# Addresses at multiples of 512 bytes for the large on-chip buffers of a two-layer decoder trunk

## The chip, the cores and the metric

The kernel runs on one core of one Trainium2 chip. The metric is the device time of one execution in microseconds (us); three runs of the kernel before took 2226.89 to 2227.21 us, median 2227.1. A core has TensorE (matrix products, PE in the profile, with its weight loads as PEld), VectorE (DVE), ScalarE (ACT), GpSimd (POOL) and SyncE (SP). The on-chip memory SBUF has 128 partitions; an address below is the byte offset within a partition, the same in all of them. Products are accumulated in another memory, PSUM.

## The reference

256 tokens of width 2048 in float32 pass two layers.

```python
h = x
for layer in range(2):
    hn = rms_norm(h, norm_mix[layer])
    if layer == 0:
        mix = recurrent_mixers(hn, ...)     # RG-LRU scan beside HGRN2 heads, then w_out
    else:
        mix = dilated_attention(hn, positions, w_qkv, w_o)   # rotary on 32 of 128 features
    h = h + mix
    h = h + relu(rms_norm(h, norm_mlp[layer]) @ w1[layer]) ** 2 @ w2[layer]
return rms_norm(h, final_norm)
```

All weights (about 410 MB) are read once. HGRN2 works in chunks by masks of a triangular recurrence; the attention turns the first 32 features of queries and keys by angles made from `positions`.

## The kernel before

*Products.* Each float32 operand is split in two float32r parts, hi (a rounded copy, ScalarE, L104) and lo (the rest, VectorE, L105), and a product is the sum of three: hi with hi, hi with lo, lo with hi. Activations stand split in `bufa` and `bufb`, 16 blocks of 128 features, each with 256 columns of hi and 256 of lo. Every product of a weight with an activation is issued on line 176, by `mm`, which keeps TensorE's order. There are two directions. `project` makes features times tokens: 128 columns of the weights' `hi` or `lo` are stationary, and a block of `bufa` moves, 512 columns (both parts) with hi, 256 with lo (`cross`, L208), or 256 three times (`direct`, L214). `tokens` and `products` make tokens times features: 128 columns of `bufa`, `bufb` or `forms` are stationary and 512 columns of `hi` or `lo` move. `forms` holds sums of blocks, with which `products` does a 2 by 2 block product of w2 in seven block products instead of eight.

*Weights.* They come as units of 1 MB, [128, 2048] float32, in a fixed order (`units`). Each goes by a transfer on SP's queue to one of three buffers `raw`, and is split to one of three `hi` and three `lo`. `fetch` runs two units ahead of use. `raw` is free for the next transfer when VectorE has written `lo`. For `products`, units are also combined: `a` and `t1` lie in a pool `pair`, opened after the recurrence, and POOL's queue adds to `t1` by a transfer (L138).

*Places.* A pool takes a range of SBUF in the order of the `tile_pool` calls, and its buffers the places in order of first use. The default is a multiple of 32 bytes; `align_bytes=LINE`, 64 here, is asked for by bufa, bufb, hi, lo and forms. Closing a pool (`mixers.close()`, `pairs.close()`) frees its range for the next, whose first writers then wait for the last users.

*Around the change.* The scan masks `msk` (L249) lie in the constants' pool and are loaded on POOL's queue at the start; the masked copies of `hgrn` (L474) read them. `nr` of pool `tmp` holds the row of inverse norms `rs` (L365), by which each projection of the layer is multiplied (L411); one buffer of this name, first for layer 0, later for layer 1. `ppi` (L726) is a buffer of the pool `rot`, opened when the recurrence's pool has been closed; positions come to it by a DMA of POOL's queue, and fifteen VectorE operations (L731 to L750) and two sines on ScalarE make `cosT` and `sinT`, which are first used in the attention. A scheduler orders each engine's instructions by its own estimate of time; `urgent` and `stream` raise a priority. `lru_gates` runs its products into three PSUM buffers `p`, which the readers (L199, L411) free again.

Of the kernel before, what the change touches and what calls it, by code (L numbers as in the profile page):

```python
# [10 lines left out]
F32 = mybir.dt.float32  # L11
F32R = mybir.dt.float32r
BF16 = mybir.dt.bfloat16
I32 = mybir.dt.int32
# [5 lines left out]
P = 128  # L20
S = 256
D = 2048
KB = D // P
EPS = 1e-6
LEVELS = (1, 2, 4, 8, 16)
NLEV = len(LEVELS)
# [14 lines left out]
def trunk_kernel(ctx, tc, x, xtok, cols, tab, masks, pos, fin, w_in, w_gate, w_out, w_qkv, w_o, w1, w2, out):  # L41
    nc = tc.nc
    pool = lambda name, bufs=1, **kw: ctx.enter_context(tc.tile_pool(name=name, bufs=bufs, **kw))
    cst = pool("cst")
    act = pool("act")
    wraw = pool("wraw", 3)
    whi = pool("whi", 3)
    wlo = pool("wlo", 3)
    tmp = pool("tmp", 2)
# [8 lines left out]
    xall = act.tile([P, KB * S], F32, name="xall")  # L58
    xin = xall.rearrange("p (k s) -> p k s", s=S)
    xres = xall.rearrange("p (j d) -> p j d", j=2)  # L60
    bufa = act.tile([P, KB, 2 * S], F32R, name="bufa", align_bytes=LINE)
    bufb = act.tile([P, KB, 2 * S], F32R, name="bufb", align_bytes=LINE)

    units = []
    made = {}
# [27 lines left out]
    class Weights:  # L93
        def __init__(self, raw, step=2048):
            self.raw = raw
            self.hi = whi.tile([P, 2048], F32R, name="hi", align_bytes=LINE)
            self.lo = wlo.tile([P, 2048], F32R, name="lo", align_bytes=LINE)
            for at in range(0, 2048, step) if step else ():
                self.split(at, step)

# [145 lines left out]
        fetch_first()  # L246
    tab_ = cst.tile([P, NTAB], F32, name="tab_")
    nc.gpsimd.dma_start(tab_, tab)
    msk = cst.tile([P, NLEV, P], mybir.dt.int8, name="msk")  # L249
    nc.gpsimd.dma_start(msk, masks)  # L250
    ident = tab_[:, TC_ID:TC_ID + P]
    lnc = tab_[:, TC_LNC:TC_LNC + 384]
    epsc = cst.tile([P, 1], F32, name="epsc")
# [168 lines left out]

    vgs = mixers.enter_context(tc.tile_pool(name="vgs", bufs=1))
    wk = mixers.enter_context(tc.tile_pool(name="wk", bufs=2))


    def halves(t, c, second):
# [150 lines left out]
    rot = mixers.enter_context(tc.tile_pool(name="rot", bufs=1))  # L578
# [140 lines left out]
    pair = pairs.enter_context(tc.tile_pool(name="pair0", bufs=1))  # L719
    forms = pair.tile([P, 4, 2, 512], F32R, name="forms", align_bytes=LINE)  # L720
    nx1 = Norm()
# [1 line left out]
    pairs.close()  # L723


    ppi = rot.tile([32, S], I32, name="ppi")  # L726
    nc.gpsimd.dma_start(ppi, bass.AP(tensor=pos.tensor, offset=pos.offset, ap=[[0, 32], [1, S]]))
    ang = rot.tile([32, S], F32, name="ang")
    cosT = rot.tile([32, S], F32, name="cosT")
# [24 lines left out]
    wk = mixers.enter_context(tc.tile_pool(name="wk2", bufs=2))  # L754
# [69 lines left out]
    pair = pairs.enter_context(tc.tile_pool(name="pair1", bufs=1))  # L824
    forms = pair.tile([P, 4, 2, 512], F32R, name="forms", align_bytes=LINE)
    fnorm = Norm()
# [25 lines left out]
URGENT = 400  # L852
ORDER = "v0 h0 x0 h1 x1 h2 x2 h3 x3 v1 h4 x4 h5 x5 h6 x6 h7 x7 g0 y0 y1 y2 y3 g1 y4 y5 y6 y7"
WARM = 12
LINE = 64
PAIRS = 2
T3_DMA = True
PRODUCTS = (("a", 0), ("t1", 4), ("n", 6), ("t2", 5), ("c", None), ("n", 7), ("t3", None), ("d", 1),
# [105 lines left out]
```

## Time and profile before

| | |
|---|---|
| median of three runs | 2227.1 us |
| the profiled execution | 2227.31 us, of which its span 2225.5 |
| instructions | 29702 |
| granted TensorE clock, mean | 0.998 |
| read from HBM | 427.48 MB, 193 GB/s over the span |
| transfers on SP's queue | 52.8% of 16 engines' span |
| VectorE, line 105 (lo) | 822.1 us |
| ScalarE, line 104 (hi) | 688.3 us |

Shares of time are of the span. The groups of the page have busy time, the mean of one, and the idle time before them with what ended it. A stretch of the chain of waits has its start, its length and what worked. In the order in time the first column is the start, the second the time until the last of the merged instructions ended; products are pipelined, so one starts before the one before has drained, and the distance between starts tells the pace. In the busy time by stretches, each engine's time has the number of its instructions behind it.

### The profile page before, as it was taken

How to read it: one execution, taken by the hardware profiler on the slowest of the kernel's cores; microseconds unless marked ns; L12 is line 12 of the kernel's file. 1: busy time of each engine (PE TensorE's matmuls, PEld its weight loads, DVE VectorE, ACT ScalarE, POOL GpSimd, SP SyncE). 2: the span in 40 equal slices, each digit the busy share in tenths (PEclk: the TensorE clock that was granted, in tenths of full speed). 3: DMA queues.
4: the chain of work that ended last, by engine and by line, in shares of the span. 5: the costliest groups of instructions: out<-in, count | busy, mean ns of one | idle time of the engine just before them, and what ended most of it. 6: DMA issues, size and time to landing. Idle time of an engine off the chain costs nothing.

```text
span 2225.5 us, 29702 instructions
## 1 busy us (share of the span) xinstructions
PE 2207.2 (99%) x12004; PEld 1892.6 (85%) x12004; DVE 1673.0 (75%) x2286; ACT 1110.0 (50%) x1364; POOL 15.8 (1%) x23
## 2 busy tenths in 40 slices
PE   9999999999999999999999999999999999999997
PEld 8999998888888888888888888888878888888886
DVE  8777796578777877877867878556787687687787
ACT  6444585444445444544654444444454454454454
POOL 0000000000000000000000000000000000000000
PEclk9999999999999999999999999999999999999999
DMA  8444446556655755755654544655566567566553
GB/s 312 163 158 163 158 154 228 180 185 203 229 187 186 242 196 174 244 199 159 208 207 158 182 173 164 224 179 185 158 218 241 171 201 247 188 189 246 190 189 114
DMA packets 61017, 431.25 MB, mean 194 GB/s; under 512 B 6784, under 2 KB 7552, under 8 KB 9424
## 3 DMA queue, kind: packets, MB, share of 16 engines
q1 hardware_dynamic: 58320, 412.20, 52.8%
q0 software_dynamic: 2560, 17.16, 4.2%
q8 instruction: 94, 1.54, 0.3%
q14 instruction: 43, 0.35, 0.0%
HBM read 427.48 MB, written 2.10 MB: 193 GB/s over the span
## 4 chain that ended last, share of the span: by engine, by line
PE 95%; DVE 3%; ACT 1%; DMA 0%; issue 0%; SPq 0%; ACTq 0%; DVEq 0%
PE p L176 81%; PE po L176 6%; PE pd L176 5%; DVE lo L105 1%; PE pl L471 1%; ACT hi L104 1%; PE pl L179 0%; DVE a L142 0%; PE pl L777 0%; PE po L798 0%; DMA xall<-in_x 0%; PE pd L790 0%; DMA a<-in_w 0%; DVE bufa L234 0%; PE pd L455 0%
## 5 line engine op out<-in xcount | busy, mean ns | idle before, releaser
L105 DVE TENSOR_TENSOR lo<-raw,hi 128x1024 fp32r<-128x1024 f32 (+2 forms) x486 | 822.1, 1709 | 359.3 <-ACT hi L104 339.2
L104 ACT CAST hi<-raw 128x1024 fp32r<-128x1024 f32 (+2 forms) x486 | 688.3, 1441 | 685.2 <-PE p L176 524.9
L176 PE MATMUL p<-bufa,hi 128*128 128x512 f32 (+1 forms) x3840 | 862.8, 359 | 2.4 <-DVE bufa L234 2.3
L176 PEld LDWEIGHTS p<-bufa,hi 128*128 128x128 f32 x3840 | 668.1, 188 | 104.8 <-DVE bufa L234 3.8
L176 PE MATMUL p<-bufa,lo 128*128 128x256 f32 x3200 | 517.6, 283 | 0.0
L176 PEld LDWEIGHTS p<-bufa,lo 128*128 128x128 f32 x3200 | 449.4, 188 | 14.2
L176 PE MATMUL p<-hi,bufb 128*128 128x512 f32 x1408 | 458.0, 395 | 0.2 <-DVE xall L650 0.2
L176 PEld LDWEIGHTS p<-hi,bufb 128*128 128x128 f32 x1408 | 264.4, 188 | 64.1 <-DVE xall L650 3.1
L176 PE MATMUL p<-lo,bufb 128*128 128x512 f32 x704 | 277.8, 395 | 0.3 <-DVE lo L105 0.2
L104 ACT CAST hi<-a 128x2048 fp32r<-128x2048 f32 x64 | 122.0, 1906 | 160.9 <-PE p L176 83.6
L105 DVE TENSOR_TENSOR lo<-a,hi 128x2048 fp32r<-128x2048 f32 x64 | 146.5, 2289 | 55.5 <-ACT hi L104 55.4
L176 PEld LDWEIGHTS p<-lo,bufb 128*128 128x128 f32 x704 | 132.1, 188 | 33.1 <-DVE lo L105 2.7
L176 PE MATMUL p<-hi,bufa 128*128 128x512 f32 x384 | 125.1, 400 | 0.4 <-ACT hi L104 0.4
L176 PEld LDWEIGHTS p<-hi,bufa 128*128 128x128 f32 x384 | 72.3, 188 | 16.7 <-ACT hi L104 1.3
L176 PE MATMUL pd<-hi,bufb 128*128 128x512 f32 x256 | 85.5, 395 | 0.1
L176 PE MATMUL po<-hi,bufb 128*128 128x512 f32 x256 | 85.4, 394 | 0.1
L176 PE MATMUL p<-hi,forms 128*128 128x512 f32 x256 | 85.4, 394 | 0.0
L176 PE MATMUL p<-lo,bufa 128*128 128x512 f32 x192 | 76.5, 399 | 1.8 <-DVE lo L105 1.8
L142 DVE TENSOR_TENSOR a<-a,raw 128x2048 f32<-128x2048 f32 x32 | 73.0, 2282 | 0.0
L223 ACT COPY t<-p 128x256 f32<-128x256 f32 x128 | 47.0, 367 | 41.4 <-PE p L176 41.1
L650 DVE SCALAR_TENSOR_TENSOR xall<-p,nm,xall 128x512 f32<-128x512 f32 x64 | 47.7, 746 | 24.7 <-PE p L176 24.7
L230 ACT CAST bufb<-zp 128x256 fp32r<-128x256 f32 x128 | 50.8, 404 | 17.2 <-DVE zp L684 17.1
(239 smaller groups left out, 1807.9 us busy)
## 6 DMA issues: line engine op xcount, KB each, us to landing
raw<-in_w SPq DMA_DIRECT2D x224, 1024.0 KB, 4.8
raw<-in_w_qkv SPq DMA_DIRECT2D x48, 1024.0 KB, 4.8
raw<-in_w_in SPq DMA_DIRECT2D x46, 1024.0 KB, 4.8
raw<-in_w_out SPq DMA_DIRECT2D x16, 1024.0 KB, 4.8
a<-in_w SPq DMA_DIRECT2D x16, 1024.0 KB, 4.8
t<-in_w SPq DMA_DIRECT2D x16, 1024.0 KB, 4.9
t<-in_w POOLq DMA_DIRECT2D x16, 1024.0 KB, 8.0
raw<-in_w_o SPq DMA_DIRECT2D x16, 1024.0 KB, 4.9
```

The lines of the kernel that those rows point to most:

```text
L104: A.copy(h, w)
L105: V.tensor_tensor(l, w, h.bitcast(F32), OP.subtract)
L142: V.tensor_tensor(r, r, held[add], OP.add)
L176: chain[:] = [after(T.matmul(*args, **kw), chain)]
L223: A.copy(t, p[:, S:])
L230: A.copy(dst[:, :S], src)
L471: T.matmul(pl[:, j], kq[:, js], halves(qp[:, js], c, True), start=True, stop=True)
L650: V.scalar_tensor_tensor(xres[:, j, at], bank, (r2 if sign > 0 else r2n)[:, j:j + 1], xres[:, j, at], op0=OP.mult, op1=OP.add)
```

## The change

LINE becomes 512, and only forms still asks for it. A buffer of 320 bytes, never used, is put ahead in the constants' pool; msk leaves that pool for the recurrence's pool `wk`, still loaded on POOL's queue, and ppi becomes the first 32 partitions of `nr`. The buffers behind then follow each other at multiples of 512 by their sizes.

```diff
     cst = pool("cst")
+    cst.tile([P, 80], F32, name="gap")
     act = pool("act")
...
-    bufa = act.tile([P, KB, 2 * S], F32R, name="bufa", align_bytes=LINE)
-    bufb = act.tile([P, KB, 2 * S], F32R, name="bufb", align_bytes=LINE)
+    bufa = act.tile([P, KB, 2 * S], F32R, name="bufa")
+    bufb = act.tile([P, KB, 2 * S], F32R, name="bufb")
...
-            self.hi = whi.tile([P, 2048], F32R, name="hi", align_bytes=LINE)
-            self.lo = wlo.tile([P, 2048], F32R, name="lo", align_bytes=LINE)
+            self.hi = whi.tile([P, 2048], F32R, name="hi")
+            self.lo = wlo.tile([P, 2048], F32R, name="lo")
...
-    msk = cst.tile([P, NLEV, P], mybir.dt.int8, name="msk")
-    nc.gpsimd.dma_start(msk, masks)
...
     wk = mixers.enter_context(tc.tile_pool(name="wk", bufs=2))
+    msk = wk.tile([P, NLEV, P], mybir.dt.int8, name="msk", bufs=1)
+    nc.gpsimd.dma_start(msk, masks)
...
-    ppi = rot.tile([32, S], I32, name="ppi")
+    ppi = tmp.tile([P, S], F32, name="nr", bufs=1)[:32].bitcast(I32)
     nc.gpsimd.dma_start(ppi, bass.AP(tensor=pos.tensor, offset=pos.offset, ap=[[0, 32], [1, S]]))
...
-LINE = 64
+LINE = 512
```

The two built programs place the buffers so (first of each name; the others of a name lie whole buffers further):

| buffer | bytes | before | past a multiple of 512 | after | past a multiple of 512 |
|---|---|---|---|---|---|
| xall | 16384 | 20800 | 320 | 20480 | 0 |
| bufa | 32768 | 37184 | 320 | 36864 | 0 |
| bufb | 32768 | 70016 | 384 | 69632 | 0 |
| raw, three | 8192 | 102784 | 384 | 102400 | 0 |
| hi, three | 8192 | 127360 | 384 | 126976 | 0 |
| lo, three | 8192 | 152000 | 448 | 151552 | 0 |
| t1 of tmp, two | 1024 | 176576 | 448 | 176128 | 0 |
| forms, layer 0 | 16384 | 187328 | 448 | 185856 | 0 |
| a, layer 0 | 8192 | 208832 | 448 | 207808 | 448 |

The instructions are the same in number on every engine. Their order differs only between the last heads of the recurrence and the first units of the output projection: the angle work begins 70 VectorE operations later and ends 4 later, the two transposes of the last head come 59 TensorE instructions earlier, a few casts and sigmoids of ScalarE change places, and on SP's queue the transfers to `a` and `t1` stand one place earlier among those of w_out.

## The prediction, made before the changed kernel ran

> **What bounds the kernel now.** I read the page's busy table first, then the chain that ended last, then the groups of instructions, and last the order in time of TensorE's products.
>
> ```profile
> PE 2207.2 (99%) x12004; PEld 1892.6 (85%) x12004; DVE 1673.0 (75%) x2286; ACT 1110.0 (50%) x1364; POOL 15.8 (1%) x23
> PEclk9999999999999999999999999999999999999999
> PE 95%; DVE 3%; ACT 1%; DMA 0%; issue 0%; SPq 0%; ACTq 0%; DVEq 0%
> ```
>
> TensorE works 2207.2 of 2225.5 us at the full granted clock in every slice, and 95% of the chain that ended last is its own work. So the end of the program is the sum of the distances from one product's start to the next. The groups of line 176 (kept apart by shape) hold those products:
>
> ```profile
> L176 PE MATMUL p<-bufa,hi 128*128 128x512 f32 x2560 | 625.9, 396 | 2.3 <-DVE bufa L234 2.3
> L176 PE MATMUL p<-bufa,lo 128*128 128x256 f32 x3200 | 517.6, 283 | 0.0
> L176 PE MATMUL p<-hi,bufb 128*128 128x512 f32 x1408 | 458.0, 395 | 0.2 <-DVE xall L650 0.2
> L176 PE MATMUL p<-hi,forms 128*128 128x512 f32 x256 | 85.4, 394 | 0.0
> ...
> L176 PE MATMUL p<-bufa,hi 128*128 128x256 f32 x1280 | 236.9, 285 | 0.1
> ```
>
> Line 176 has 6784 products of 512 columns: 2560 with bufa as the moving side, 2880 with bufb as the stationary side, 768 with forms and 576 with bufa (the smaller groups of these names included). Another 4576 have 256 columns. The means above overlap and include the drain, so I take the pace from starts. The order in time of TensorE, first column the start in us, gives it in four places:
>
> ```profile
> 608.74 3.19 PE L176 MATMUL p<-bufa,hi 128*128 128x512 f32 x13
> 611.77 2.06 PE L176 MATMUL p<-bufa,lo 128*128 128x256 f32 x16
> 613.66 0.62 PE L176 MATMUL p<-bufa,hi 128*128 128x512 f32 x2
> ```
> ```profile
> 706.77 0.40 PE L176 MATMUL p<-hi,forms 128*128 128x512 f32 x1
> ...
> 709.58 0.40 PE L176 MATMUL p<-hi,bufb 128*128 128x512 f32 x1
> ...
> 715.14 0.40 PE L176 MATMUL pd<-hi,forms 128*128 128x512 f32 x1
> ```
> ```profile
> 1408.88 0.39 PE L176 MATMUL p<-lo,bufa 128*128 128x512 f32 x1
> ...
> 1414.42 0.39 PE L176 MATMUL p<-lo,bufa 128*128 128x512 f32 x1
> ```
>
> - bufa moving, hi stationary, 512 columns: (611.77 - 608.74) / 13 = 233.1 ns each.
> - bufa moving, lo stationary, 256 columns: (613.66 - 611.77) / 16 = 118.1 ns.
> - forms stationary: 12 products from 706.77 to 709.58, 234.2 ns.
> - bufb stationary: 24 products from 709.58 to 715.14, 231.7 ns.
> - bufa stationary: 24 products from 1408.88 to 1414.42, 230.8 ns.
>
> No engine held TensorE up in these runs, and the last three do the same work: 512 columns of hi and lo pass 128 columns of the stationary buffer. What differs is the stationary buffer and where it lies: forms begins 448 bytes past a multiple of 512, bufb 384, bufa 320. With hi at 384, lo at 448 and bufa at 320, every 512-byte stationary slice in the kernel lies across two 512-byte blocks, and every 2048-byte moving slice across five.
>
> **The change part by part.**
>
> *The addresses.* xall, bufa, bufb, raw, hi, lo and forms go to multiples of 512. No instruction of line 176 is added or removed, so the whole effect is a change of pace. After it each stationary slice lies in one block and each 2048-byte moving slice in four. The trace of before has no product on such an address, so I bound the price from both sides. The gain: 3.4 ns lie between the slowest and the fastest of the three alike runs (234.2 - 230.8), and the order of those runs is the order of the bytes before the first block boundary (64, 128, 192 bytes); a slice with no boundary would be at or past the fast end. The far bound of the gain is TensorE's pace without any such loss. A row near to that is the pair of float32 products below, 256 columns at (1423.75 - 1423.32) / 2 = 215 ns per record, the fastest long step of the trace; 233 - 215 = 18 ns a product would be 6784 x 18 + 4576 x 9 = 163 us.
>
> ```profile
> 1423.32 0.59 PE L798 MATMUL po<-pT,vg 128*128 128x256 f32 x2
> 1423.75 0.59 PE L798 MATMUL pd<-pT,vg 128*128 128x256 f32 x2
> ```
>
> The loss: every product as slow as the slowest run, 234.2. I take the near end of the gain, all 512-column products at 230.8, since that pace is measured on the same kind of operands and the far bound is of another type: 2560 x 2.3 + 2880 x 0.9 + 768 x 3.4 + 576 x 0 = 5.9 + 2.6 + 2.6 = 11.1 us. For 256 columns I take half of the first difference, 4576 x 1.15 = 5.3 us. Together 16.4 us.
>
> The Trainium skill's TensorE page (TensorE: Matmul & The Clock Gate, Back-to-back issue gap) has an isolated gap of N/2.4 + 2.5 ns, 216 ns for 512 columns, with no term for the address. The trace disagrees with it by 15 to 18 ns (230.8 to 234.2); were all of that lost to addresses, the estimate from that page would be 6784 x 16 + 4576 x 9 = 150 us of gain.
>
> *Not all of it reaches the end.* Once in each quarter of the two feed-forward stages TensorE waits for a chain that runs on ScalarE, VectorE and a transfer:
>
> ```profile
> 715.34 1.91 ACT hi L104
> ...
> 719.60 5.05 DMA a<-in_w
> ...
> 729.01 2.30 DVE a L142
> ...
> 740.76 5.59 PE p L176 x23
> ```
>
> From 715.34 to 740.76 the chain of waits passes over no product, so a quicker TensorE gains nothing there. The pair pool loads its buffer a sixteen times, twice in a quarter, and I take one such stretch for each of the eight quarters:
>
> ```profile
> a<-in_w SPq DMA_DIRECT2D x16, 1024.0 KB, 4.8
> ```
>
> Eight stretches of 25.4 us are 203 us, 9% of the span; the gain is 16.4 x 0.91 = 14.9 us. In the first 21 us TensorE waits for x and the first weights, and the masks' transfer keeps its place:
>
> ```profile
> 2.12 5.32 DMA xall<-in_x
> ```
> ```profile
> 1.96 0.57 POOL L250 DMA_DIRECT2D msk<-in_masks  x1
> ```
> ```profile
> L474 DVE COPY_PREDICATED st<-msk,pl x40: 283/298/454, 54.8 to 282.7; 128x128 f32<-128x128 int8 x40
> ```
>
> *The masks.* One DMA of 80 KB, still second on POOL's queue behind the table; first read at 54.8 us, 50 us after it lands. Price nothing; without that cover it would be its own landing, some 5 us.
>
> *The positions' temporary.* ppi becomes the buffer nr, which holds the scale of layer 0, so its DMA on POOL waits for the last product with rs instead of for the freed pool. The fifteen angle operations on VectorE (L731 to L750) that follow begin 70 places later on VectorE, around 338 us instead of 303, and end at the same place; their number is unchanged. On POOL nothing but the later weight transfers is queued behind that DMA. VectorE loses the burden where TensorE waits today:
>
> ```profile
> 303.46 0.27 DVE L731 CAST ang<-ppi 32x256 f32<-32x256 int32 x1
> ...
> 305.88 0.41 DVE L411 TENSOR_TENSOR z<-p,nr 128x256 f32<-128x256 f32 x1
> ```
> ```profile
> 306.98 0.47 ACT L199 ACTIVATE gr<-p,c__82 128x256 f32<-128x256 f32 x1
> ```
> ```profile
> 306.34 0.51 PE L176 MATMUL p<-bufb,hi 128*128 128x256 f32 x2 [0.98 <-DVE z L411]
> ...
> 307.50 0.50 PE L176 MATMUL p<-bufb,hi 128*128 128x256 f32 x2 [0.18 <-ACT gr L199]
> ```
>
> The product that frees a bank for line 176 (L411) stands behind four of the angle operations and would be about 1 us earlier. What is late next is the sigmoid gr on ScalarE, which begins at 306.98 us behind the weight casts of its queue and ends the second wait above; so of the 0.98 us I count 0.1; bounds 0 and 1.2 us. Where the work lands, in the output projection, VectorE has room:
>
> ```profile
> 350.00:430.00 80.00, 80.00 (x366) 65.33 (x365) 42.74 (x45) 37.86 (x53) 0.00 (x0) 1.00 0.56 199
> ```
>
> TensorE is never idle in these 80 us and VectorE is for 37. Without that cover the angle work costs its own length, 5 us (four of L741 and eleven of some 0.3).
>
> ```profile
> L741 DVE SCALAR_TENSOR_TENSOR ang<-cosT,ang 32x256 f32<-32x256 f32 x4 | 1.6, 406 | 0.0
> ```
>
> *The queue of SP.* The first transfer of the pair pool (a, L129) is issued one place earlier, ahead of a load of w_out:
>
> ```profile
> 309.60 34.41 SPq L121 DMA_DIRECT2D raw<-in_w_out  x7
> 345.65 0.33 SPq L129 DMA_DIRECT2D a<-in_w  x1
> ```
> ```profile
> 345.17 0.41 DVE L565 TENSOR_TENSOR z<-z,xc 128x256 f32<-128x256 f32 x1
> ...
> 350.97 2.00 ACT L104 CAST hi<-raw 128x1024 fp32r<-128x1024 f32 x2 [3.06 <-PE p L176]
> ```
>
> It waits for the recurrence's last reader (L565, done at 345.58). The seventh load, issued at 344.0 at the latest (309.60 + 34.41), would go out some 2 us later, and land about 4.8 us after that; ScalarE reads it at 350.97 at the earliest because TensorE's buffers come free then. Price nothing; without the cover 2 us.
>
> *Sum.* The profiled run took 2227.3 us, 1.8 outside its span, against a median of 2227.1. 2227.3 - 14.9 - 0.1 = 2212.3; I say 2212.
>
> **The rivals.**
>
> *The place within 512 bytes does not matter* (no change). For it: 448 and 320 are both 64 past a multiple of 128, yet forms and bufa are the slow and the fast run, and the two slices that forms and bufb alternate between lie 2048 and 1024 bytes apart, which could be the cause as well. Then all paces stay: 2227.3 - 0.1 = 2227.
> The Trainium skill's SBUF page (SBUF — State Buffer, Specifications) knows only 16-byte lines, which every address here already respects, so by that page nothing moves; the trace has 2.5 ns between two such runs.
>
> *Equal offsets collide* (slower). After the change the moving and the stationary slice always begin at the same place in a block, so TensorE's two reads run in step. For it: the slowest run contains the pair lo and forms, both at 448. Against it: hi and bufb, both at 384, run at 231.7. If all products take forms' pace, 2560 x 1.1 + 2880 x 2.5 + 576 x 3.4 + 4576 x 0.55 = 2.8 + 7.2 + 2.0 + 2.5 = 14.5 us, 2242; if only the equal pair is slow, and a third of the run carries all of the 2.5 ns, it is 7.5 ns a product, 6784 x 7.5 + 4576 x 3.7 = 68 us, 2295. It decides from 0.4 ns a product (4.5 us over 11360).
>
> *The order stalls TensorE* (slower). The angle work or the later load empties the queue of weights: 5 us, 2232.
>
> **How the numbers follow.** Forecast 0.43, no effect 0.26, collision 0.28, order 0.03. About 0.2%, 4.5 us, is what a measurement of this kernel can tell from no change; so faster 0.43, same 0.26, slower 0.31. The forecast's own range runs from 2170 (a third of the far bound of 163 us) to 2222. The whole range is 2170 to 2252: it leaves out a gain beyond a third of the far bound, and a collision that costs more than about a fifth of the way from 2242 to 2295.
>
> **What would show it.** The three runs of 24 products: if bufb, forms and bufa as stationary buffers come out within 1 ns of each other and at or under 231 ns, the step on addresses is right; if they stay at 231.7, 234.2 and 230.8 the first rival is. Any of them over 236 is the collision. TensorE's wait for L411 near 306 us should shrink and none appear between 340 and 430 us. The prediction is wrong if the time leaves 2170 to 2252, or if the time changes while the paces do not.

## The result and the profile after

The changed kernel takes 2206.81 us (median of four runs, 2206.44 to 2207.46) where the kernel before takes 2227.14 beside it: a ratio of 0.9909, with a 95% interval of 0.9892 to 0.9926. That is 20.3 us less, 5 below the forecast. The profiled execution has a span of 2205.2 us at a clock of 0.998. Its lines of code stand one lower (L176 is L177). First the page's busy times and its chain of waits by engine, after the change:

```profile
PE 2181.3 (99%) x12004; PEld 1898.5 (86%) x12004; DVE 1673.5 (76%) x2286; ACT 1109.8 (50%) x1364; POOL 15.8 (1%) x23
...
PE 83%; DVE 10%; ACT 3%; DMA 2%; issue 1%; SPq 0%; ACTq 0%; DVEq 0%
```

The number of products is the same and TensorE is as full as before, so its products follow each other faster. But of the chain that ended last, TensorE's share fell from 95% to 83% of the span; VectorE's rose from 3% to 10%, ScalarE's from 1% to 3%, that of transfers from 0 to 2%. The groups of the products, kept apart by shape, after the change:

```profile
L177 PE MATMUL p<-bufa,hi 128*128 128x512 f32 x2560 | 615.0, 392 | 2.4 <-DVE bufa L235 2.4
L177 PE MATMUL p<-bufa,lo 128*128 128x256 f32 x3200 | 522.2, 285 | 0.0
L177 PE MATMUL p<-hi,bufb 128*128 128x512 f32 x1408 | 451.9, 391 | 1.3 <-DVE xall L651 1.3
...
L177 PE MATMUL p<-bufa,hi 128*128 128x256 f32 x1280 | 239.7, 287 | 0.1
```

Compare with the same groups of before: the products of 512 columns are busy for less time (625.9 to 615.0, 458.0 to 451.9 us), and those of 256 columns for more (517.6 to 522.2, 236.9 to 239.7). The paces come from the order in time of TensorE after the change, in a projection and in a feed-forward stage:

```profile
606.19 3.82 PE L177 MATMUL p<-bufa,hi 128*128 128x512 f32 x16
609.85 2.08 PE L177 MATMUL p<-bufa,lo 128*128 128x256 f32 x16
611.76 0.63 PE L177 MATMUL p<-bufa,hi 128*128 128x512 f32 x2
```
```profile
703.77 0.39 PE L177 MATMUL p<-hi,forms 128*128 128x512 f32 x1
...
706.49 0.39 PE L177 MATMUL p<-hi,bufb 128*128 128x512 f32 x1
...
711.93 0.39 PE L177 MATMUL pd<-hi,forms 128*128 128x512 f32 x1
```

12 products with forms take (706.49 - 703.77) / 12 = 226.7 ns each (before 234.2), 24 with bufb (711.93 - 706.49) / 24 = 226.7 (before 231.7), 16 of bufa with hi (609.85 - 606.19) / 16 = 228.8 (before 233.1). The 16 of bufa with lo take 119.4 (before 118.1). Not all of this reaches the end. What TensorE waited for, in us in total, times, and the longest, before and then after:

```profile
PE p L176 <- DVE lo L105: 2.0, 5, 0.8
...
PE p L176 <- DVE xall L650: 0.2, 1, 0.2
```
```profile
PE p L177 <- DVE lo L106: 5.8, 11, 0.8
...
PE p L177 <- DVE xall L651: 1.3, 8, 0.2
```

The waits for the next split weights and for the residual's update are the ones that grow; over all rows of these two tables TensorE's idle time goes from 7.2 to 12.2 us.

And one stage has become slower. In 108 us of the input projections of layer 0, where the products of weights have 256 columns, the number of TensorE instructions falls from 915 to 911, with no idle time in either (before, then after):

```profile
32.00:140.00 108.00, 108.00 (x915) 107.65 (x915) 79.72 (x192) 50.84 (x88) 0.00 (x0) 1.00 0.55 195
```
```profile
32.00:140.00 108.00, 108.00 (x911) 107.87 (x910) 79.35 (x191) 49.61 (x87) 0.00 (x0) 1.00 0.55 195
```

### The profile page after: what moved, and what is told of

Its sections match the earlier page's. It is cut to its first block, busy times and chain, and to the rows that moved or that the text cites. A ratio compares the mean times of both kernels' runs of the same rounds, so it can differ in the third digit from the quotient of the medians.

```text
span 2205.2 us, 29703 instructions
## 1 busy us (share of the span) xinstructions
PE 2181.3 (99%) x12004; PEld 1898.5 (86%) x12004; DVE 1673.5 (76%) x2286; ACT 1109.8 (50%) x1364; POOL 15.8 (1%) x23
## 3 DMA queue, kind: packets, MB, share of 16 engines
q0 software_dynamic: 2560, 17.16, 4.3%
## 4 chain that ended last, share of the span: by engine, by line
PE 83%; DVE 10%; ACT 3%; DMA 2%; issue 1%; SPq 0%; ACTq 0%; DVEq 0%
PE p L177 75%; DVE lo L106 5%; PE po L177 5%; DVE a L143 3%; ACT hi L105 3%; DMA a<-in_w 2%; PE pd L177 1%; PE pl L472 1%; DVE xall L651 1%; PE pl L180 0%; PE pl L778 0%; DVE bufa L235 0%; PE po L799 0%; DMA xall<-in_x 0%; PE pd L791 0%
## 5 line engine op out<-in xcount | busy, mean ns | idle before, releaser
L177 PE MATMUL p<-bufa,hi 128*128 128x512 f32 (+1 forms) x3840 | 854.7, 357 | 2.4 <-DVE bufa L235 2.4
L177 PEld LDWEIGHTS p<-bufa,hi 128*128 128x128 f32 x3840 | 672.2, 190 | 95.1 <-DVE bufa L235 3.8
L177 PE MATMUL p<-bufa,lo 128*128 128x256 f32 x3200 | 522.2, 285 | 0.0
L177 PEld LDWEIGHTS p<-bufa,lo 128*128 128x128 f32 x3200 | 452.8, 192 | 12.7
L177 PE MATMUL p<-hi,bufb 128*128 128x512 f32 x1408 | 451.9, 391 | 1.3 <-DVE xall L651 1.3
L177 PEld LDWEIGHTS p<-hi,bufb 128*128 128x128 f32 x1408 | 264.5, 188 | 58.8 <-DVE xall L651 4.7
L177 PE MATMUL p<-lo,bufb 128*128 128x512 f32 x704 | 275.2, 391 | 4.2 <-DVE lo L106 4.2
L177 PEld LDWEIGHTS p<-lo,bufb 128*128 128x128 f32 x704 | 132.3, 188 | 34.1 <-DVE lo L106 7.6
L177 PE MATMUL p<-hi,bufa 128*128 128x512 f32 x384 | 123.7, 397 | 0.2 <-ACT hi L105 0.2
L177 PEld LDWEIGHTS p<-hi,bufa 128*128 128x128 f32 x384 | 72.4, 188 | 15.5 <-ACT hi L105 1.0
L177 PE MATMUL pd<-hi,bufb 128*128 128x512 f32 x256 | 84.3, 390 | 0.2 <-DVE xall L651 0.2
L177 PE MATMUL po<-hi,bufb 128*128 128x512 f32 x256 | 84.2, 390 | 0.2 <-DVE xall L651 0.2
L177 PE MATMUL p<-hi,forms 128*128 128x512 f32 x256 | 84.1, 389 | 0.0
L177 PE MATMUL p<-lo,bufa 128*128 128x512 f32 x192 | 76.2, 397 | 1.7 <-DVE lo L106 1.6
```

Of the source, the lines that this page charges most:

```text
L177: chain[:] = [after(T.matmul(*args, **kw), chain)]
```

## The experiments

In the tables below a pace is the mean distance in ns from one product's start to the next, over all unbroken runs of nine or more products of a kind in the profiled execution; for 256 columns in the order hi, hi, lo (`direct`), over all distances under 140 ns. Places are bytes past a multiple of 512. "Distance" is the place of the stationary slice minus that of the moving one.

**The moves without the addresses.** The masks and the positions' temporary move as in the change; a buffer of 128 bytes keeps the places of before.

```diff
     cst = pool("cst")
+    cst.tile([P, 32], F32, name="gap")
...
-    msk = cst.tile([P, NLEV, P], mybir.dt.int8, name="msk")
-    nc.gpsimd.dma_start(msk, masks)
...
     wk = mixers.enter_context(tc.tile_pool(name="wk", bufs=2))
+    msk = wk.tile([P, NLEV, P], mybir.dt.int8, name="msk", bufs=1)
+    nc.gpsimd.dma_start(msk, masks)
...
-    ppi = rot.tile([32, S], I32, name="ppi")
+    ppi = tmp.tile([P, S], F32, name="nr", bufs=1)[:32].bitcast(I32)
```

> The masks and the positions' temporary are moved as in the change, but the buffers keep their places of before (xall and bufa 320, bufb, raw and hi 384, lo and forms 448 bytes past a multiple of 512). If the gain comes from the addresses: 2227 us as before, paces of the three runs of 24 products as before (bufb 231.7, forms 234.2, bufa 230.8 ns as stationary side). If the moved masks, positions and order bring it: 2207 us as after.

2227.63 us, ratio 1.0002 (0.9993 to 1.0012), paces of before. What TensorE waited for in this kernel:

```profile
PE p L177 <- DVE lo L106: 1.9, 5, 0.8
...
PE p L177 <- ACT gr L200: 0.7, 1, 0.7
PE p L177 <- DVE z L410: 0.4, 1, 0.4
```

So the moves are worth nothing that this interval (0.2% wide) can show, and the waits for lo do not come from them: with the old paces they are the old 2 us. The gain of 20 us is the addresses'.

**All places equal, but not at multiples of 512.** Two kernels shift everything, by the buffer in the constants' pool and by LINE.

```diff
-    cst.tile([P, 80], F32, name="gap")
+    cst.tile([P, 96], F32, name="gap")
...
-LINE = 512
+LINE = 64
```

> The changed kernel with xall, bufa, bufb, raw, hi, lo and forms all 64 bytes past a multiple of 512, so all offsets are equal, and every 512-byte slice lies across two blocks. If the place in the 512-byte block decides: about 2227 us, paces 231 to 234 ns. If only equal offsets of the moving and the stationary slice matter: 2207 us and paces of 226.7 ns as after. If the unit is 64 bytes: 2207 us too, but then before should not have been slower, as its buffers lie at multiples of 64.

The other has 16 in place of 96 elements, and LINE = 256:

> The changed kernel with the same seven buffers all 256 bytes past a multiple of 512. If blocks of 512 decide: about 2227 us, 231 to 234 ns. If blocks of 256 or less, or equal offsets: 2207 us, 226.7 ns.

2207.54 us (ratio 0.9912, 0.9897 to 0.9927) and 2206.96 us (0.9910, 0.9895 to 0.9925). At 64 every stationary slice lies across two blocks and every moving one across five, as before the change, and the order in time of TensorE is that of after:

```profile
606.15 3.82 PE L177 MATMUL p<-bufa,hi 128*128 128x512 f32 x16
609.81 2.08 PE L177 MATMUL p<-bufa,lo 128*128 128x256 f32 x16
611.72 1.55 PE L177 MATMUL p<-bufa,hi 128*128 128x512 f32 x6
```

(609.81 - 606.15) / 16 = 228.8 ns. The forecast's mechanism, that a slice across two blocks costs time, falls here; what remains is the distance between the two sides.

**hi, lo and forms 128 bytes away from bufa and bufb.** A buffer of 128 bytes ahead of the pool of hi, and LINE = 128.

```diff
+    pool("gap1").tile([P, 32], F32, name="gap1")
     whi = pool("whi", 3)
...
-LINE = 512
+LINE = 128
```

> The changed kernel with hi, lo and forms 128 bytes past a multiple of 512; xall, bufa, bufb and raw at multiples of it. In the projections hi and lo are the stationary side (bufa moves), in the feed-forward stages they are the moving side (bufb, bufa stationary). If both sides' places count: 2227 us, all paces over 230. If only the stationary slice's place counts: the runs with bufb stationary keep 226.7 ns and those with bufa moving go back to 233, about 2216 us. If only the moving slice's place counts, the other way round, about 2219 us. If a place at a multiple of 128 is enough: 2207 us.

2227.57 us, ratio 1.0002 (0.9993 to 1.0012). The time alone would have fitted "both sides' places count". The order in time tells more:

```profile
707.31 0.39 PE L178 MATMUL p<-hi,forms 128*128 128x512 f32 x1
...
710.04 0.41 PE L178 MATMUL p<-hi,bufb 128*128 128x512 f32 x1
...
715.63 0.39 PE L178 MATMUL pd<-hi,forms 128*128 128x512 f32 x1
```

forms, at 128 like hi and lo, takes (710.04 - 707.31) / 12 = 227.5 ns, though both its sides lie across blocks; bufb, inside its blocks but 128 away from hi and lo, takes (715.63 - 710.04) / 24 = 232.9.

**The distance by itself.** A program without the model passes runs of 64 products over one moving and one stationary buffer, and changes only the two places.

```python
def s(k, off):
    at = off // 4 + k % 16 * 128
    return st[:, at:at + 128]
def m(k, off, n):
    at = off // 4 + k % 16 * 512
    return mov[:, at:at + n]
...
for k in range(64): on(T.matmul(to(k, 512), s(k, 64), m(k, 0, 512), **acc(k, 512)))
```

> The whole model is left out: the program loads x, copies it to a moving buffer and a stationary buffer, and passes runs of 64 products over them, one run for each pair of offsets. Slices follow each other by 2048 bytes (moving) and 512 bytes (stationary), as in the projections. Line 78 warms up with 512 products; lines 79 to 88 have 512 columns, the moving side at 0 and the stationary side at 0, 16, 32, 64, 128, 192, 256, 320, 384, 448 bytes past a multiple of 512; lines 89 to 91 the moving side at 64, 128, 256 and the stationary at 0; line 92 both at 64; line 93 both at 0 again. Lines 94 to 103 have 256 columns: stationary at 0, 16, 32, 64, 128, 256, 384 with the moving side at 0; moving at 128 with stationary at 0; both at 64; both at 0. If the distance of the two sides modulo 512 decides by itself: lines 79, 92 and 93 take 226.7 ns a product, all other lines of 512 columns 231 to 234; lines 94, 102 and 103 take 120 ns, the other lines of 256 columns 118 to 119. If the unit is smaller, lines at multiples of it are fast too (256: lines 85 and 91). If the distance matters only beside the other engines' traffic: 226.7 in all lines of 512 columns.

In its order in time each row is one run, and the distance to the next row's start over 64 is the pace:

```profile
132.31 14.67 PE L79 MATMUL p<-mov,st 128*128 128x512 f32 x64
146.82 14.68 PE L80 MATMUL p<-mov,st 128*128 128x512 f32 x64
...
176.25 15.09 PE L82 MATMUL p<-mov,st 128*128 128x512 f32 x64
191.19 15.04 PE L83 MATMUL p<-mov,st 128*128 128x512 f32 x64
206.06 14.82 PE L84 MATMUL p<-mov,st 128*128 128x512 f32 x64
220.72 14.67 PE L85 MATMUL p<-mov,st 128*128 128x512 f32 x64
235.22 15.09 PE L86 MATMUL p<-mov,st 128*128 128x512 f32 x64
...
323.75 14.71 PE L92 MATMUL p<-mov,st 128*128 128x512 f32 x64
338.30 14.68 PE L93 MATMUL p<-mov,st 128*128 128x512 f32 x64
352.82 7.83 PE L94 MATMUL p<-mov,st 128*128 128x256 f32 x64
360.49 7.74 PE L95 MATMUL p<-mov,st 128*128 128x256 f32 x64
...
375.63 7.42 PE L97 MATMUL p<-mov,st 128*128 128x256 f32 x64
382.89 7.75 PE L98 MATMUL p<-mov,st 128*128 128x256 f32 x64
390.48 7.84 PE L99 MATMUL p<-mov,st 128*128 128x256 f32 x64
```

512 columns: 226.7 ns at distance 0, 233.4 at 64, 232.3 at 128, 229.1 at 192 and again 226.6 at 256; both sides at 64 (L92) 227.3. 320, 384 and 448, in rows not shown, repeat 64, 128 and 192 within 0.2 ns. With the moving side shifted by 64 and 128 instead, distances -64 and -128, also in rows not shown, it is 229.2 and 232.3, the paces of 192 and 128. So the period is 256 bytes, not 512, and no other engine is needed for the effect. 256 columns: 119.8 at 0, but 113.4 at 64 and 118.6 at 128. So equal places are good for 512 columns and bad for 256, which is why the stage of `direct` lost in the change.

**The period in the kernel.** hi, lo and forms 256 bytes from bufa and bufb.

```diff
-    cst.tile([P, 80], F32, name="gap")
...
+    pool("gap1").tile([P, 64], F32, name="gap1")
     whi = pool("whi", 3)
...
-LINE = 512
+LINE = 64
```

> The changed kernel with xall, bufa, bufb and raw 192 bytes past a multiple of 512, and hi, lo and forms at 448: all moving slices are 256 bytes away from the stationary ones modulo 512, no two are at the same place in a 512-byte block, and none at a multiple of 128. If the distance modulo 256 decides, as the sweeps say: 2207 us, paces as after (bufb 227.0, forms 226.7, bufa with hi 228.4, with lo 119.5 ns). If the same place in a 512-byte block is needed beside the other engines' traffic: 2227 us, paces over 231.

2207.54 us (0.9911, 0.9894 to 0.9927), all paces within 0.1 ns of after's. Nothing here lies at a multiple of 128.

**lo alone.** lo stands at another place than hi and the rest: 128 bytes further in one kernel, 64 in another (everything else at 256 or 0).

```diff
-    cst.tile([P, 80], F32, name="gap")
+    cst.tile([P, 16], F32, name="gap")
...
+    pool("gap1").tile([P, 32], F32, name="gap1")
     wlo = pool("wlo", 3)
...
-LINE = 512
+LINE = 256
```

> The changed kernel with xall, bufa, bufb, raw and hi 256 bytes past a multiple of 512, lo at 384 and forms at 0. If the distance between the moving and the stationary slice decides: products of bufa with hi (512 columns, projections) keep 228.4 ns, those of bufa with lo (256 columns) go back to 118.7, and of the runs of 24 with bufb as the stationary side, 8 of 24 have lo moving and lose 5 ns each, so a mean of 228.6; forms differs from both and goes to 231 or more. In all 2880 x 1.7 + 768 x 5 + 576 x 1.7 = 9.7 us lost and 3.7 us won, of which two thirds reach the end: about 2211 us. If all buffers have to agree at once for any gain: 2227 us.

The other has 16 in place of 32 elements ahead of wlo:

> The changed kernel with lo alone 64 bytes further than the rest modulo 256 (xall, bufa, bufb, raw, hi at 256, lo at 320, forms at 0), the distance at which the first sweep had 113.3 ns for 256 columns in place of 120. If each product goes by its own distance: 3200 products with lo stationary gain 6 ns, the 1408 with lo moving (distance 192) lose 2.2, net 16 us, two thirds of it at the end: about 2196 us, faster than both. If the mixture of two distances spoils the runs with lo moving as it did with lo at 128 bytes: bufb and forms at 229 to 231.5 ns, 10 to 20 us lost there, 2200 to 2215 us.

2219.65 us (0.9966, 0.9954 to 0.9979) and 2213.14 us (0.9938, 0.9921 to 0.9954). The first missed its expectation of 2211 by 9 us, and the second lies in the range expected for a mixture that spoils the runs. The paces of the kernels of the model so far, without those whose paces are the same as in a row shown:

| distances of hi / lo to bufa | bufb stationary | forms stationary | bufa with hi, 512 | bufa with lo, 256 | `direct`, 256 | us |
|---|---|---|---|---|---|---|
| before (64 / 128) | 232.0 | 234.4 | 232.9 | 118.7 | 118.2 | 2227.1 |
| all equal (after) | 227.0 | 226.7 | 228.4 | 119.5 | 119.8 | 2206.8 |
| 256 / 256 | 227.1 | 226.7 | 228.4 | 119.5 | 119.8 | 2207.5 |
| 128 / 128 | 232.5 | 227.6 | 232.8 | 118.7 | 119.0 | 2227.6 |
| 0 / 128 | 231.5 | 231.2 | 227.5 | 120.3 | 119.1 | 2219.7 |
| 0 / 64 | 232.0 | 231.9 | 228.5 | 117.6 | 117.9 | 2213.1 |

In the last two rows only one of three products in the feed-forward runs has lo moving, and hi still stands at distance 0 to bufb, yet the whole run takes 231.5 to 232.0. A pace is not a sum over products by their own distances: one product in three that stands elsewhere slows all three.

**The sequences by themselves.** The second sweep tries more distances and the kernel's own sequences.

> The model is left out as in the first sweep; only the distance (stationary minus moving, bytes) varies, with one moving and two stationary buffers (hi, lo). Line 91 warms up. Lines 92 to 101: 512 columns at distances 48, 80, 96, 112, 144, 160, 176, 208, 224, 240. Lines 102 to 112: 256 columns at 48, 80, 96, 112, 144, 160, 176, 192, 208, 224, 240. Lines 113 to 116: the order of the projections (16 products of 512 columns with hi, then 16 of 256 with lo) at distances of hi and lo of 0 and 0 (after), 0 and 64, 64 and 128 (before), 64 and 64. Lines 117 to 120: the other projection order (hi, hi, lo, 256 columns each) at the same four. Lines 121 to 123: the order of the feed-forward stages (hi, lo, hi moving, 512 columns) with hi and lo at 0 and 0 (after), 0 and 64, 64 and 64 past the stationary side. If the pace depends on the distance modulo 256: 512 columns at 226.7 near 0 and 240, 229 to 233 between; 256 columns 113 to 114 near 64 and 118 to 120 elsewhere; lines 113 and 121 as after (228.4 and 119.5; 227), line 115 as before (232.9 and 118.7), line 114 with 113 to 114 for its products of 256 columns. If the mixture decides (each product's pace depends on those before it): line 114 near line 113 and line 122 as slow as 231.

With 512 columns 240 is as good as 0 (227.1), and 48, 80, 96, 112, 144, 160, 176, 208 and 224 take 230 to 234.2; with 256 columns none of the other distances comes under 116.7. The kernel's sequences come out as in the kernel, with nothing else running. Here are the order of the projections at 0 and 0 (L113) and at 64 and 64 (L116), and the range of starts of the feed-forward order with hi at 0 and lo at 64 (L122):

```profile
280.00 3.82 PE L113 MATMUL p<-mov,sth 128*128 128x512 f32 x16
283.66 2.08 PE L113 MATMUL p<-mov,stl 128*128 128x256 f32 x16
285.58 3.82 PE L113 MATMUL p<-mov,sth 128*128 128x512 f32 x16
...
350.65 2.05 PE L116 MATMUL p<-mov,stl 128*128 128x256 f32 x16
352.53 3.90 PE L116 MATMUL p<-mov,sth 128*128 128x512 f32 x16
356.27 1.98 PE L116 MATMUL p<-mov,stl 128*128 128x256 f32 x16
358.09 3.89 PE L116 MATMUL p<-mov,sth 128*128 128x512 f32 x16
```
```profile
L122 PE MATMUL p<-sth,mov x64: 387/393/402, 436.0 to 458.1; 128*128 128x512 f32 x64
```

L113: (283.66 - 280.00) / 16 = 228.8 and (285.58 - 283.66) / 16 = 120.0 ns, the 228.8 and 119.4 of after. L122: 95 distances in 22.1 us, about 232 ns, as in the kernel with lo at 64 (232.0); after the first, second and third product of a triple the mean distance is 231.0, 231.9 and 232.9 ns, so all three are slow, not only the one with lo. And L116 shows the history: the same 16 products at the same addresses take (352.53 - 350.65) / 16 = 117.5 ns once and (358.09 - 356.27) / 16 = 113.8 the next time.

**A version that beats both.** In layer 0, up to the recurrence's output projection, the view of bufa begins 64 bytes lower, so that the 1920 products of `direct` have distance 64.

```diff
-    cst.tile([P, 80], F32, name="gap")
+    cst.tile([P, 16], F32, name="gap")
...
-    bufa = act.tile([P, KB, 2 * S], F32R, name="bufa")
+    act.tile([P, 48], F32, name="gapa")
+    abuf = act.tile([P, KB * 2 * S + 16], F32R, name="bufa")
+    bufa = abuf[:, :KB * 2 * S].rearrange("p (k s) -> p k s", s=2 * S)
...
+    bufa = abuf[:, 16:].rearrange("p (k s) -> p k s", s=2 * S)
     nrm = out_project(w_out, "nmlp0", (2, 3, 0, 1))
```

> The changed kernel, but in layer 0 up to the recurrence's output projection the view of bufa begins 64 bytes below a multiple of 512 (in everything later at a multiple of it), so that hi and lo stand 64 bytes past the moving slice for the 1920 products of 256 columns of that stage. By the sweeps they take 113.3 ns in place of 120, 12.8 us in all, and the 192 products with bufa as the stationary side 228.9 in place of 226.7, 0.4 us lost. If the stage is bound by these products: 2195 to 2199 us, faster than both kernels. If VectorE and ScalarE bound the stage once the products are faster: 2203 to 2207 us. If the sweeps' pace does not hold beside the other engines' traffic: 2207 us with 118 to 120 ns.

2201.02 us (2200.22 to 2201.48), ratio to before 0.9881 (0.9865 to 0.9898): with before at 2227.39 beside it. That is 5.8 us under the changed kernel, between two of the expected ranges. The intervals of the two ratios touch (0.9892 and 0.9898), but every run of this kernel is shorter than every run of the changed one (2206.44 to 2207.46). The stretch shown above for before and after, now in this kernel:

```profile
32.00:140.00 108.00, 108.00 (x924) 107.50 (x923) 81.14 (x192) 52.12 (x92) 0.00 (x0) 1.00 0.55 195
```

924 instructions in place of 911, and VectorE at 81 of 108 us does not bound the stage. The products take 115.8 ns on average, not the 113.4 of the sweep: most unbroken runs keep to one of two rhythms, 113.5 to 114 or 117.8 ns, as L116 does. What puts a run into one or the other is open. 1920 x (119.8 - 115.8) = 7.7 us, of which 5.8 reach the end.

## Why the prediction was right or wrong

*The addresses: the mechanism was wrong, and the gain was there for another reason.* The step "a slice with no boundary would be at or past the fast end" is refuted by the kernels with everything at 64, and at 192 and 448: every slice lies across blocks, and the paces are those of after. What counts is the distance between the moving and the stationary slice modulo 256 bytes. The order of the three runs by their bytes ahead of a boundary (64, 128, 192), on which the step rested, was a coincidence of three points, and partly of the run chosen: over all unbroken runs before, bufb and bufa as stationary sides stand at 232.0 and 231.7, almost the same. The runs also differed in distance: forms stood at 64 and 0 to hi and lo, bufb at 0 and -64, bufa at -64 and -128, and none had both at 0.

*Its sizes.* By the table, 512 columns gained 2880 x 5.0 + 768 x 7.7 + 2560 x 4.5 + 576 x 3.4 (231.7 to 228.3 with bufa stationary) = 33.8 us, where 11.1 were forecast: the pace of 230.8 was the fastest slow case, not the new pace. 256 columns lost 2560 x 0.8 + 1920 x 1.6 = 5.1 us where 5.3 of gain were forecast; "half of the first difference" had no row behind it and had the wrong sign. Net 28.7 against 16.4.

*"Not all of it reaches the end."* The stretches were named rightly, but they were read from the chain of one window, and the term was too small: 20.3 of 28.7 us arrived, 0.71 and not 0.91. In the chain of the whole program before, such a stretch with a transfer of `a` stands once (at 719.60 us), and 95% of that chain is TensorE's own work, which leaves 111 us, not 203, for all else. Only with the quicker products is there one in each of the eight quarters, the second of them like this:

```profile
703.94 8.17 PE p L177 x36
...
716.40 4.62 DMA a<-in_w
...
737.13 5.53 PE p L177 x23
```

Of the 8.4 us given back, 5.0 are the growth of TensorE's idle time shown above; it is absent at the old paces, with the moved masks and positions in place. From start to start it is more, because the product after a wait does not overlap the one before it (the longest wait of this kind after the change: 793 ns idle, 1182 ns from start to start). In the products with bufb stationary, the distances over 300 ns take 22.2 us (46 of them) in place of 14.1 (40), and what they hold above the mean pace grows by 6.9 us. The other 1.5 of the 8.4 us were not taken apart; 0.7 of them lie behind the start of the last product.

*The masks, the positions and SP's order* were priced at 0, 0.1 and 0 us, and the kernel with these alone is within 0.12% of before. The wait near 306 us, in the order in time after the change:

```profile
307.45 0.50 PE L177 MATMUL p<-bufb,hi 128*128 128x256 f32 x2 [0.27 <-DVE z L410]
...
309.15 0.51 PE L177 MATMUL p<-bufb,hi 128*128 128x256 f32 x2 [0.72 <-ACT gr L200]
```

0.98 + 0.18 became 0.27 + 0.72: what the projection's reader gave, the sigmoid behind it took, as the forecast had it, and 0.17 us is left. In the output projection TensorE is still busy for 80.00 of the 80 us from 350 to 430, so VectorE's room did hide the angle work.

*The rivals.* "The place within 512 bytes does not matter" was half true: it does not, but the distance does. "Equal offsets collide" had the right two things, the two sides' places against each other, and the wrong sign for 512 columns; for 256 it was right (119.8 against 118.2 and 113.4). It was held off by hi and bufb, both at 384, running at 231.7; that run has lo at 448 in every third product, and the runs with lo alone moved show that this is enough to make all of it slow.

*The test that was named* (three runs within 1 ns of each other and under 231) was met: forms and bufb take 226.7 ns, and the run with bufa that stood at 230.8 takes (1403.53 - 1398.08) / 24 = 227.1.

```profile
1398.08 0.40 PE L177 MATMUL p<-lo,bufa 128*128 128x512 f32 x1
...
1403.53 0.39 PE L177 MATMUL p<-lo,bufa 128*128 128x512 f32 x1
```

By its own rule the step on addresses would have passed as right, and the time of 2206.81 us lies in the forecast's range; that it came out faster is luck as far as the cause goes. The change sets both the places in the block and the distances; only kernels that set one without the other could tell.

The Trainium skill's formula, on TensorE: Matmul & The Clock Gate, Back-to-back issue gap, gives by its N/2.4 + 2.5 an isolated gap of 215.8 ns for 512 columns and 109.2 for 256. No steady run here reached either: the lowest are 226.7 and 113.4, at distances 0 and 64.

## What to carry to other kernels

Where products follow each other without a gap, try the distance between the moving and the stationary operand's places modulo 256 bytes, separately for each number of columns and on the real sequence, in a small program that holds nothing else: here 0 is best for 512 columns and 64 for 256. Keep all operands of one sequence at one distance, since here one odd product in three slowed all three. And expect part of a faster pace back as waits on the engines that feed it.

## What the runs showed that was not expected

- The pace of a steady run depends on the distance of its two operands with a period of 256 bytes: 226.7 to 234.2 ns for 512 columns (0, 16 and 240 are the fast ones), 113.4 to 120 for 256. With all seven buffers at one place, it does not matter which of the three tried it is (0, 64 or 256: 2206.8 to 2207.5 us).
- The pace has a memory. After products of 256 columns the first products of 512 columns at distance 0 are slower (228.8 as the mean of 16, against 226.7 in long runs), and the same run took 113.8 or 117.5 ns by what went before it. Why the two sides' distance matters at all, the traces do not show; this stays open.
